# Half of the last additions on POOL, split channel sums for the second half, and row factors transposed later, in one encoder layer

## The chip, the cores and the metric

The kernel runs on one core of a Trainium2 chip. Its engines work side by side, each with its own queue of instructions: TensorE (PE in the profile; its weight loads are PEld), VectorE (DVE), ScalarE (ACT), GpSimd (POOL) and SyncE (SP), which here only issues DMAs. PE writes its products to PSUM, a small memory of banks of 128 x 512 float32; everything else lies in SBUF. POOL takes no part in reading PSUM here.

The metric is the time of one execution in microseconds on the device. Profiled executions have a time of their own.

## The reference

One layer of an encoder for 1024 tokens of 1024 channels, all in float32. The input is normed over its channels and goes through one projection into a pooling branch (u) and into q, k and v of an attention; both branches are gated and merged, projected, normed again and added to the input. A squared-ReLU MLP follows in the same frame:

```python
h = rmsnorm(x, g_pre_mix)
proj = jnp.einsum('bsd,de->bse', h, w_in)            # u_pool | q | k | v
...
mix = jnp.einsum('bsd,de->bse', merged, w_out)
x = x + rmsnorm(mix, g_post_mix)
h2 = rmsnorm(x, g_pre_mlp)
a = jnp.square(jax.nn.relu(jnp.einsum('bsd,df->bsf', h2, w_up)))
ff = jnp.einsum('bsf,fd->bsd', a, w_down)
x = x + rmsnorm(ff, g_post_mlp)
```

`rmsnorm` divides each token by the root of the mean of its squares over the 1024 channels. There are four of these norms, and the change touches all four.

## The kernel before

**Layout.** Activations lie with channels on the partitions: eight tiles of 128 channels by 512 tokens for each half (h = 0 and 1) of the tokens. A product in float32 is made from three products of split operands: a matrix is cast to a shorter type (fp32r) by ACT, the "hi" part, and DVE subtracts it from the original to get the "lo" part; `mm3` (L112 to L114, L110 where an issue order is pinned) multiplies hi by hi, hi by lo and lo by hi. A step of `dense_steps` is three such matmuls of 128 x 512; eight steps make one output tile.

**Norms.** For a norm the squares of the eight channel tiles are added up (acc) and then summed over the partitions by a matmul with a matrix `ones`, all 1/1024 (tile ms). This product is a plain float32 one, which the profile shows as two instructions. `rstd` (L151 to L157) makes the row factor from it: a logarithm and an exponential on ACT and three instructions on DVE. The result is the same in all 128 partitions and goes to `rb[h]`.

**Stage 1** (`phase_in`). Squares and splits of x; then the products of u, groups 0 to 2, for half 0 and then half 1, and group 3 for both halves. The function `stats(h)` makes the row factors (L332 for the sum) and then four transposes of `rb[h]` (L336, tile rt), out of which DVE copies one column each (L337) into `rcol`, the row factors with tokens on the partitions, as v needs them. Both sums and both sets of transposes use a PSUM tile with the tag "o", of which there is one buffer. `stats` is handed to the products of half 1 as side work, `stats(0)` after 2 of their 24 steps and `stats(1)` after 14. After that `u_out` (L380) multiplies the products of u by `rb` on the way out of PSUM; `pool_group` and `pool_mix` make the pooling branch on DVE and PE (tile dm, first half also tag "o"; evicted at L418 and L419). Products for q and k follow, then v (L496, L497), gates and the attention.

**Norm chain** (`chain`, one per half). After the projection of the mixer, each half goes through two norms: sum at L826, scaling and residual (L834, L838), sum at L846, scaling (L851). For half 1 the operands of the MLP are built from the results on DVE and ACT (L877 to L884, L811, L812). It is side work of the first MLP products, whose weights are loaded, cast and split in between (L76, L82, L83).

**Last stage** (`down`). Seven series of products; DVE and ACT split their operands two units ahead (L1091, L1093, L1102). The last norm is in `norm(h, ...)`: sums of `accs` and of the last square (L1200, L1201), row factor, scaling (L1213), residual addition (L1218) and the store (L1219). Half 1 runs as side work beside the series q4 and p2. Half 0 comes last and in two parts of 256 tokens, whose final four products are in `last_tokens`; the second of these parts has nothing beside it any more. The residual of half 0 was loaded ahead into SBUF.

**Order.** The kernel is written for a planner: it traces the instructions, and the planner orders them for each engine by a list schedule in its own model of the time, where the order of the program is the priority. Edges by hand (`issue_after`) fix some orders. Each engine then works its queue off strictly in that order. The constants: `ones` is filled by a memset at the start; then a tile of zeros is filled, from which nine matmuls run ahead of the first real one.

Of the kernel before, what the change touches and what calls it, by code (L numbers as in the profile page):

```python
# [29 lines left out]
P = 128  # L30
H = 512
# [18 lines left out]
class Block:  # L50
# [106 lines left out]
        nc.vector.scalar_tensor_tensor(out=y, in0=b, scalar=-3.0, in1=y, op0=ALU.add, op1=ALU.mult)  # L157
        return y

    def split_gain(self, src, gain, r, hi, lo, pool):  # L160

        nc = self.nc
        n = src.shape[-1]
        f = pool.tile([P, H], F32, name="nf", tag="nf", bufs=4)[:, :n]
        nc.vector.scalar_tensor_tensor(out=f, in0=src, scalar=gain, in1=r, op0=ALU.mult, op1=ALU.mult)
        nc.scalar.copy(hi, f)
        nc.vector.tensor_sub(lo, f, hi.bitcast(F32))

    def build(self):
        tc, nc = self.tc, self.nc  # L170
        self.table_inst = None
        order = [(("u", g), O_U + g) for g in (0, 1, 2, 3)]
        order += [(("q", 0), O_QK), (("k", 0), O_QK + 1)]
        self.fill = {
# [10 lines left out]
        }  # L185
        order += [(("v", 0, j), O_V + j) for j in range(2)]
        for h in range(-1, 9):
            for f in self.fill[h]:
                if f[0] == "v":
                    if f[1] == 0:  # L190
                        order += [(("v", 1, j), O_V + 2 + j) for j in range(2)]
                elif f[0] == "g":
                    if f[-1] != 1 or len(f) == 2:
                        order.append((f[:2], O_G + f[1]))
                else:
                    order.append((f, O_QK + 2 * f[1] + (f[0] == "k")))
        order += [(("br", e), O_BR + e) for e in range(8)]
        kept = {3: "t2_hi", 4: "t2_lo"}
        order += [(("out", 0, e), O_OUT + e, (), None, kept.get(e)) for e in range(8)]
        order += [(("out", 1, e), O_OUT + e) for e in (2, 1, 0)]  # L200
        order += [(("up", i), O_UP + self.pair(i)[0]) for i in range(16)]
        self.set_order(order)

        cp = tc.alloc_tile_pool(name="const", bufs=1, side="left")
        self.wp = tc.alloc_tile_pool(name="weights", bufs=1, side="left")
        self.big = tc.alloc_tile_pool(name="big", bufs=1, side="left")
        dp = tc.alloc_tile_pool(name="scratch", bufs=1, space=DRAM)
        self.gscr = [dp.tile([P, 1024], F32, name=f"gscr{i}") for i in range(16)]
        self.yscr = [[dp.tile([P, 1024], F32R, name=f"yscr{i}_{j}") for j in range(2)] for i in range(4)]
        self.pscr = [[dp.tile([P, 4, H], F32, name=f"pscr{i}_{j}") for i in range(4)] for j in range(2)]  # L210
        self.ascr = [[dp.tile([P, 4, H], F32, name=f"ascr{f}_{h}") for h in range(2)] for f in range(8)]
        self.tscr = [dp.tile([P, 4, H], F32, name=f"tscr{f}") for f in range(4)]
        self.wscr = [[dp.tile([P, 4, 512], F32, name=f"wscr{n}_{q}") for q in range(4)] for n in range(4)]
        self.wsums = self.weight_sums()
        self.xscr = [[dp.tile([P, H], F32, name=f"xscr{h}_{e}") for e in range(8)] for h in range(2)]

        self.vt = cp.tile([P, N_VEC], F32, name="vt")
        nc.scalar.preload_act_table_set(TABLES)
        self.ones = cp.tile([P, P], F32, name="ones")
        nc.vector.memset(self.ones, 1.0 / 1024.0)  # L220
        self.one1 = cp.tile([P, 1], F32, name="one1")
        nc.vector.memset(self.one1, 1.0)
        self.eps = cp.tile([P, 1], F32, name="eps")
        nc.vector.memset(self.eps, EPS)
        self.gn = cp.tile([P, 32], F32, name="gn")
        self.eye = cp.tile([P, P], F32, name="eye")

        self.past = cp.tile([P, 1024], mybir.dt.uint8, name="past")
        self.rcnt = cp.tile([P, 16], F32, name="rcnt")

        self.rp = tc.alloc_tile_pool(name="row", bufs=1, side="left")
        self.rb = [self.rp.tile([P, H], F32, name=f"rb{h}") for h in range(2)]
        self.rcol = cp.tile([P, NK], F32, name="rcol")
        edge = tc.alloc_tile_pool(name="edge", bufs=1, side="right")
        self.edge = edge.tile([P, 24], F32, name="edge")
        self.dps = tc.alloc_tile_pool(name="att_d", bufs=2, space=PSUM)
        self.zps = tc.alloc_tile_pool(name="att_z", bufs=1, space=PSUM)
        self.phase_in()
        self.phase_attention()
        self.phase_post()  # L240
        self.phase_mlp()

        edge.release()
        for p in (self.rp, self.big, self.wp, cp, dp):
            p.release()


    def phase_in(self):
        tc, nc = self.tc, self.nc
        pa = tc.alloc_tile_pool(name="in_a", bufs=1, side="right")  # L250
        xs = [pa.tile([P, NK, H], F32, name=f"x{h}") for h in range(2)]

        def load(h, k, n):
            nc.sync.dma_start(xs[h][:, k : k + n, :], self.x[h][:, k : k + n, :])
# [75 lines left out]
        def stats(h):  # L330
            ms = self.zps.tile([P, H], F32, name="ms", tag="o", bufs=1)
            nc.tensor.matmul(ms, self.ones, accs[h], start=True, stop=True)  # L332
            self.rstd(ms, pa, ("sq", 3), out=self.rb[h])
            rt = self.zps.tile([P, H], F32, name="rt", tag="o", bufs=1)
            for j in range(4):
                nc.tensor.transpose(rt[:, j * P : j * P + P], self.rb[h][:, j * P : j * P + P], self.eye)  # L336
            nc.vector.tensor_copy(  # L337
                self.rcol[:, 4 * h : 4 * h + 4].rearrange("p (j o) -> p j o", o=1),
                rt.rearrange("p (j o) -> p j o", o=P)[:, :, 0:1],
            )  # L340
# [87 lines left out]
        for h in range(2):  # L428
            d = self.dps.tile([P, H], F32, name="du", tag="d")
            self.dense(d, self.weights(("u", 3)), self.hT[h])  # L430
            u_out(3, [(h, d)])
            if h == 0:
                pool_mix(0, pooled[0])
                pooled.append(pool_group(1))
                u_out(2, list(enumerate(dst[2])))
        self.run(self.job_qk("q", 0, 0))
        pool_mix(1, pooled[1])
        pooled.append(pool_group(2))
# [375 lines left out]
    def chain(self, ch, h, mix, acc):  # L814
# [8 lines left out]
        tmp = self.hp.tile([P, 4, H], F32, name=f"tmp{h}", tag="t3_hi")  # L823
        yield 3
        ms = self.ps.tile([P, H], F32, name="ms", tag="ms", bufs=1)
        nc.tensor.matmul(ms, self.ones, acc, start=True, stop=True)  # L826
        r = self.rstd(ms, ch, None, bufs=1, b=tmp[:, 3, :])
        acc2 = ch.tile([P, H], F32, name="acc2", bufs=1)
        for e in range(8):
# [13 lines left out]
                nc.vector.tensor_add(acc2, acc2, sq)  # L843
        yield 28
        ms = self.ps.tile([P, H], F32, name="ms", tag="ms", bufs=1)
        nc.tensor.matmul(ms, self.ones, acc2, start=True, stop=True)  # L846
        self.rstd(ms, ch, None, out=self.rb[h], b=tmp[:, 3, :])

        def norm(e):
# [192 lines left out]
    def down(self):  # L1042
# [149 lines left out]
            nc.gpsimd.dma_start(t, self.xscr[h][e])  # L1192
            return t

        def norm(h, x1, gap, c=slice(0, H), behind=(None,)):

            at = gap
            yield at
            ms = self.ps.tile([P, H], F32, name="ms", tag="ms", bufs=1)[:, c]
            nc.tensor.matmul(ms, self.ones, accs[h][:, c], start=True, stop=False)  # L1200
            nc.tensor.matmul(ms, self.ones, last[h], start=False, stop=True)  # L1201
            r = self.rb[h][:, c]
            self.rstd(ms, mp, ("r", 4), n=c.stop - c.start, out=r)
            nxt = None if x1 else residual(h, 0)
            for e in range(8):
                at += gap
                yield at
                if x1:
                    x = x1[e][:, c]
                else:  # L1210
                    x, nxt = nxt, residual(h, e + 1) if e < 7 else None
                t = ff[h][e][:, c]
                nc.vector.scalar_tensor_tensor(  # L1213
                    out=t, in0=t, scalar=self.gn[:, V_POST_MLP + e : V_POST_MLP + e + 1], in1=r,
                    op0=ALU.mult, op1=ALU.mult,
                )
                with after(behind[0] if e > 2 else None):
                    nc.vector.tensor_add(t, t, x)  # L1218
                (nc.sync if h == 1 or e % 2 or behind[0] else nc.scalar).dma_start(self.out[h, e][:, c], t)  # L1219

        def last_tokens(c, ops, side):
# [50 lines left out]
        side, behind = None, [None]  # L1272
        for c in (slice(0, 256), slice(256, H)):
            last_tokens(c, ops, side)
            side = norm(0, x0, 0, c, behind)
        self.run(side)
        mp.release()

# [47 lines left out]
```

## Time and profile before

| | |
|---|---|
| median of 3 runs | 1290.21 us (1290.13 to 1290.51) |
| profiled execution, its own time | 1291.31 us |
| its span | 1289.5 us |
| instructions | 16851 |
| PE busy | 1268.3 us (98%) |
| DVE busy | 924.2 us (72%) |
| ACT busy | 605.5 us (47%) |
| POOL busy | 175.2 us (14%) |
| mean granted TensorE clock | 0.994 |

A row of a timeline gives the start in us from the beginning of the span, the time it took, engine, line, operation, and the tiles as out<-in with their shapes; rows that follow each other on an engine with the same line are merged, with their number behind an x. In square brackets stands how long the engine was idle before it and what ended that. Rows of the chain of waits have a start, a duration and what the time went to. In the waits view a row names who waited, for whom, the total in us, how often, and the longest. A row of the sums by stretch has the stretch, its length, and then for PE, PEld, DVE, ACT and POOL the busy time with the number of instructions, the granted clock of TensorE, the DMA share and the GB/s. Matmuls overlap in the pipeline, so it is the distance of their starts that counts and not the duration of one.

### The profile page before, as it was taken

The page shows a single profiled execution, that of the slowest core. Times are in us where ns is not written, and L with a number is a line of the kernel's source. Part 1 is how long each engine was busy: PE and PEld are TensorE (multiplying, and loading weights), DVE is VectorE, ACT ScalarE, POOL GpSimd, SP SyncE. Part 2 cuts the span into 40 slices and gives each one's busy share as a digit, 9 for nine tenths or more (in the row PEclk, how much of TensorE's full clock was granted, in tenths as well). Part 3 has the DMA queues.
Part 4 walks back from the last instruction along what each step waited for, and adds up shares of the span by engine and source line. Part 5 has one row for each costly group of instructions (what it writes and reads, how often), then busy time and mean ns, then how long its engine had stood idle before and what let it go on. Part 6 is the DMA issues. An engine that isn't in the chain of part 4 may idle for free.

```text
span 1289.5 us, 16851 instructions
## 1 busy us (share of the span) xinstructions
PE 1268.3 (98%) x6145; PEld 1063.1 (82%) x6145; DVE 924.2 (72%) x1303; ACT 605.5 (47%) x989; POOL 175.2 (14%) x346
## 2 busy tenths in 40 slices
PE   9899999999999999999999999999999999999996
PEld 6688888998888888888877888888888888888885
DVE  8686587688777756661667979777775655776876
ACT  8145455555555543232446646545554433344341
POOL 1011213202322331000101002211220000001000
PEclk9899999999999999999999999999999999999998
DMA  6152646624837978451338577756569546547641
GB/s 223 50 176 81 225 123 164 131 67 113 214 123 177 296 204 234 158 180 49 136 109 285 184 249 254 244 190 210 190 226 342 186 157 225 190 173 246 239 160 66
DMA packets 75746, 233.72 MB, mean 181 GB/s; under 512 B 8624, under 2 KB 11184, under 8 KB 73488
## 3 DMA queue, kind: packets, MB, share of 16 engines
q1 hardware_dynamic: 47936, 143.64, 33.8%
q0 software_dynamic: 27152, 88.49, 23.1%
q8 instruction: 48, 0.79, 0.3%
q10 hardware_dynamic: 576, 0.52, 0.1%
q14 instruction: 34, 0.28, 0.1%
HBM read 178.10 MB, written 83.89 MB: 203 GB/s over the span
## 4 chain that ended last, share of the span: by engine, by line
PE 88%; DVE 6%; DMA 2%; issue 2%; ACT 1%; SPq 0%; POOL 0%; DVEq 0%; POOLq 0%; ACTq 0%
PE d L114 18%; PE d L112 18%; PE d L113 18%; PE dg L110 5%; PE dg L114 5%; PE dg L113 5%; PE o L606 3%; PE at L581 2%; PE dqk L113 2%; PE dqk L114 2%; PE dqk L110 2%; DMA wraw<-w 2%; PE z L552 1%; PE z L549 1%; DVE wlo L83 1%
## 5 line engine op out<-in xcount | busy, mean ns | idle before, releaser
L113 PE MATMUL d<-blo,whi 128*128 128x512 f32 (+1 forms) x456 | 172.7, 379 | 0.0
L114 PE MATMUL d<-bhi,wlo 128*128 128x512 f32 (+1 forms) x456 | 171.9, 378 | 0.0
L112 PE MATMUL d<-bhi,whi 128*128 128x512 f32 (+1 forms) x456 | 168.4, 378 | 0.0
L562 DVE TENSOR_TENSOR_SCAN F<-F,past 128x384 f32<-128x384 f32 (+3 forms) x96 | 93.5, 974 | 25.8 <-ACT F L553 24.9
L82 ACT CAST whi<-wraw 128x512 fp32r<-128x512 f32 (+1 forms) x88 | 67.7, 799 | 88.5 <-PE d L113 33.9
L110 PE MATMUL dg<-hT_hi,whi 128*128 128x512 f32 x256 | 103.3, 404 | 0.3 <-DVE v L497 0.3
L83 DVE TENSOR_TENSOR wlo<-wraw,whi 128x512 fp32r<-128x512 f32 (+1 forms) x88 | 78.2, 907 | 34.1 <-ACT whi L82 34.1
L113 PE MATMUL dg<-hT_lo,whi 128*128 128x512 f32 x256 | 100.6, 393 | 0.0
L114 PE MATMUL dg<-hT_hi,wlo 128*128 128x512 f32 x256 | 100.4, 392 | 0.0
L113 PEld LDWEIGHTS d<-blo,whi 128*128 128x128 f32 x456 | 85.7, 188 | 16.3 <-issue 0.2
L114 PEld LDWEIGHTS d<-bhi,wlo 128*128 128x128 f32 x456 | 85.8, 188 | 16.0 <-issue 0.2
L112 PEld LDWEIGHTS d<-bhi,whi 128*128 128x128 f32 x456 | 85.5, 188 | 15.9
L553 ACT ACTIVATE F<-z 128x384 f32<-128x384 f32 (+3 forms) x96 | 47.3, 493 | 64.1 <-DVE T L566 38.4
L113 PE MATMUL d<-b_lo,whi 128*128 128x512 f32 x196 | 76.7, 391 | 0.0
L112 PE MATMUL d<-b_hi,whi 128*128 128x512 f32 x196 | 75.6, 390 | 0.0
L114 PE MATMUL d<-b_hi,wlo 128*128 128x512 f32 x196 | 75.3, 392 | 0.1
L1093 DVE TENSOR_TENSOR wlo<-slots_hi,whi 128x1024 fp32r<-128x1024 f32 x29 | 35.5, 1224 | 52.6 <-ACT whi L1091 52.5
L1091 ACT CAST whi<-slots_hi 128x1024 fp32r<-128x1024 f32 x29 | 30.5, 1051 | 84.5 <-PE d L113 64.9
L589 DVE TENSOR_TENSOR alo<-at,ahi 128x512 fp32r<-128x512 f32 (+1 forms) x80 | 50.6, 633 | 26.6 <-ACT ahi L588 25.9
L1091 ACT CAST whi<-slots_lo 128x1024 fp32r<-128x1024 f32 x27 | 28.4, 1052 | 72.9 <-PE d L113 59.2
L566 DVE TENSOR_TENSOR T<-T,F 128x127 f32<-128x127 f32 (+4 forms) x96 | 53.1, 556 | 10.2 <-POOL T L556 4.2
L1093 DVE TENSOR_TENSOR wlo<-slots_lo,whi 128x1024 fp32r<-128x1024 f32 x27 | 33.0, 1222 | 36.7 <-ACT whi L1091 36.7
(305 smaller groups left out, 3335.2 us busy)
## 6 DMA issues: line engine op xcount, KB each, us to landing
wraw<-w SPq DMA_DIRECT2D x80, 512.0 KB, 4.3
wscr<-w POOLq DMA_DIRECT2D x24, 1024.0 KB, 9.4
ext_b<-ascr SPq DMA_DIRECT2D x40, 512.0 KB, 4.4
gscr<-gs POOLq DMA_DIRECT2D x32, 256.0 KB, 4.6
gate<-gscr POOLq DMA_DIRECT2D x16, 512.0 KB, 3.7
pscr<-p SPq DMA_DIRECT2D x32, 256.0 KB, 3.7
braw<-w SPq DMA_DIRECT2D x16, 512.0 KB, 5.4
ascr<-c POOLq DMA_DIRECT2D x32, 256.0 KB, 5.2
```

Of the source, the lines that this page charges most:

```text
L82: nc.scalar.copy(hi[:, c], raw[:, c])
L83: self.last_lo = nc.vector.tensor_sub(lo[:, c], raw[:, c], hi[:, c].bitcast(F32)).ins
L110: nc.tensor.matmul(ps, wh, rh, start=first and i == 0, stop=False)
L112: nc.tensor.matmul(ps, wh, rh, start=first and i == 0, stop=False)
L113: nc.tensor.matmul(ps, wh, rl, start=False, stop=False)
L114: nc.tensor.matmul(ps, wl, rh, start=False, stop=last and i == n - 1)
L553: nc.scalar.activation(f[:, c : c + n], z[:, :n], AF.Sigmoid, scale=-1.0)
L562: nc.vector.tensor_tensor_scan(fr, fr, past[:, c : c + n][:, ::-1], 1.0 if top else f[:, c + n : c + n + 1], ALU.mult, ALU.max)
L566: nc.vector.tensor_mul(tl[:, c:e], tl[:, c:e], f[:, c + 1 : e + 1])
L589: nc.vector.tensor_sub(lo[:, c0:], at[:, c0:], hi[:, c0:].bitcast(F32))
L1091: last_split[0] = nc.scalar.copy(hi, src).ins
L1093: last_split[1] = nc.vector.tensor_sub(lo, src, hi.bitcast(F32)).ins
```

## The change

1. The transposes of the row factors and the copies into `rcol` leave `stats(h)` and become `columns(h)`. Both calls stand after the products of u's group 3, ahead of the first product of q.
2. `ones` becomes a tile of type fp32r, filled by a copy from a float32 tile `mean`, so that it serves split products; the float32 products read it through a view. A new helper `channel_sum` casts the sum of squares to hi on ACT, subtracts on DVE for lo, and makes two matmuls with `ones`. For half 1 it takes the place of the float32 product in both norms of the chain and in the last norm; there the last square is first added to the others on DVE, and one sum takes the place of two.
3. In the second part of half 0 of the last norm (`last_part`), the residual additions of tiles 0 to 3 are issued on POOL; those of tiles 4 to 7 stay on DVE. The stores keep their queues: odd tiles on SP, even tiles on ACT in this part.
4. The unused `split_gain` and `one1` (a memset of one column) are gone.

```diff
+    def channel_sum(self, ps, acc, pool, tag, bufs):
+        nc = self.nc
+        hi, lo = (pool.tile([P, H], F32R, name=f"acc_{n}", tag=tag, bufs=bufs) for n in ("hi", "lo"))
+        nc.scalar.copy(hi, acc)
+        nc.vector.tensor_sub(lo, acc, hi.bitcast(F32))
+        nc.tensor.matmul(ps, self.ones_r, hi, start=True, stop=False)
+        nc.tensor.matmul(ps, self.ones_r, lo, start=False, stop=True)
...
-        self.ones = cp.tile([P, P], F32, name="ones")
-        nc.vector.memset(self.ones, 1.0 / 1024.0)
-        self.one1 = cp.tile([P, 1], F32, name="one1")
-        nc.vector.memset(self.one1, 1.0)
+        self.ones_r = cp.tile([P, P], F32R, name="ones")
+        self.ones = self.ones_r.bitcast(F32)
...
+        mean = pa.tile([P, P], F32, name="mean")
+        nc.vector.memset(mean, 1.0 / 1024.0)
+        nc.vector.tensor_copy(self.ones_r, mean)
...
             self.rstd(ms, pa, ("sq", 3), out=self.rb[h])
+
+        def columns(h):
+
             rt = self.zps.tile([P, H], F32, name="rt", tag="o", bufs=1)
...
                 u_out(2, list(enumerate(dst[2])))
+        for h in range(2):
+            columns(h)
         self.run(self.job_qk("q", 0, 0))
...
-        nc.tensor.matmul(ms, self.ones, acc, start=True, stop=True)
+        if h == 0:
+            nc.tensor.matmul(ms, self.ones, acc, start=True, stop=True)
+        else:
+            self.channel_sum(ms, acc, ch, "nf", 2)
...
-        nc.tensor.matmul(ms, self.ones, acc2, start=True, stop=True)
+        if h == 0:
+            nc.tensor.matmul(ms, self.ones, acc2, start=True, stop=True)
+        else:
+            self.channel_sum(ms, acc2, ch, "nf", 2)
...
-            nc.tensor.matmul(ms, self.ones, accs[h][:, c], start=True, stop=False)
-            nc.tensor.matmul(ms, self.ones, last[h], start=False, stop=True)
+            if h == 0:
+                nc.tensor.matmul(ms, self.ones, accs[h][:, c], start=True, stop=False)
+                nc.tensor.matmul(ms, self.ones, last[h], start=False, stop=True)
+            else:
+                nc.vector.tensor_add(accs[h], accs[h], last[h])
+                self.channel_sum(ms, accs[h], mp, "r", 4)
...
-                    nc.vector.tensor_add(t, t, x)
+                    (nc.gpsimd if last_part and e < 4 else nc.vector).tensor_add(t, t, x)
...
-            side = norm(0, x0, 0, c, behind)
+            side = norm(0, x0, 0, c, behind, c.stop == H)
```

More of the change, by code (lines that the diff above doesn't have):

```diff
@@ L158, in rstd @@
         return y
-    def split_gain(self, src, gain, r, hi, lo, pool):
+    def channel_sum(self, ps, acc, pool, tag, bufs):
         nc = self.nc
[L163 to L167, printed above, removed]
+        hi, lo = (pool.tile([P, H], F32R, name=f"acc_{n}", tag=tag, bufs=bufs) for n in ("hi", "lo"))
[3 more added lines that the diff above has]
+        nc.tensor.matmul(ps, self.ones_r, lo, start=False, stop=True)
     def build(self):
@@ L1193, in residual, with norm @@
             return t
-        def norm(h, x1, gap, c=slice(0, H), behind=(None,)):
+        def norm(h, x1, gap, c=slice(0, H), behind=(None,), last_part=False):
             at = gap
```

## The prediction

> **What bounds the kernel now.** I read the page first, then the waits of TensorE alone, then the sums by stretch, then the timelines of the four places that the diff touches.
>
> ```profile
> span 1289.5 us, 16851 instructions
> PE 1268.3 (98%) x6145; PEld 1063.1 (82%) x6145; DVE 924.2 (72%) x1303; ACT 605.5 (47%) x989; POOL 175.2 (14%) x346
> ...
> PE rt L336 <- DVE rb L157: 4.6, 1, 4.6
> PE dv L112 <- DVE v L497: 0.4, 1, 0.4
> ...
> 40.00:50.00 10.00, 5.45 (x19) 3.93 (x19) 5.82 (x9) 2.15 (x3) 0.00 (x0) 0.79 0.29 98
> 50.00:60.00 10.00, 10.00 (x40) 8.05 (x39) 9.86 (x18) 1.05 (x1) 0.00 (x0) 0.87 0.01 2
> ```
>
> TensorE (PE) is busy for 98% of the span, so a microsecond comes off only if a PE wait goes, PE work goes, or the tail behind PE gets shorter. The waits view gives one wait of note: PE stands 4.6 us before the transposes of L336. The stretches around it are the only ones between 10 and 1270 us, of those I summed, with a granted clock under 1.00 (0.79 and 0.87).
>
> **Row factors transposed later.** The timeline, engine by engine:
>
> ```profile
> 29.77 0.69 DVE L155 SCALAR_TENSOR_TENSOR nb<-ms,rb 128x512 f32<-128x512 f32 x1
> 30.37 0.68 DVE L328 TENSOR_TENSOR acc<-acc,sq 128x512 f32<-128x512 f32 x1
> 36.38 0.60 PE L336 MATMUL rt<-eye,rb 128*128 128x128 f32 x4
> 37.02 0.16 DVE L337 COPY rcol<-rt 128x4 f32<-128x4 f32 x1 [3.50 <-PE rt L336]
> 41.40 1.02 PE L332 MATMUL ms<-acc,ones 128*128 128x512 f32 x2
> 42.50 0.40 PE L114 MATMUL zu<-hT_hi,wlo 128*128 128x512 f32 x1
> 46.70 0.69 DVE L157 SCALAR_TENSOR_TENSOR rb<-nb,rb 128x512 f32<-128x512 f32 x1
> 47.31 1.28 DVE L380 TENSOR_TENSOR u<-du,rb 128x512 f32<-128x512 f32 x2
> 47.45 1.11 PE L336 MATMUL rt<-eye,rb 128*128 128x128 f32 x4 [4.55 <-DVE rb L157]
> 48.21 0.77 PE L112 MATMUL du<-hT_hi,whi 128*128 128x512 f32 x1
> 52.63 0.40 PE L113 MATMUL du<-hT_lo,whi 128*128 128x512 f32 x1
> 52.87 0.40 PE L114 MATMUL du<-hT_hi,wlo 128*128 128x512 f32 x1
> ```
>
> Taking the transposes out of PE's queue would alone bring almost nothing: the next matmul, du at 48.21, needs the bank that L380 frees at about 47.31 + 0.65 = 47.96, and L380 waits for the same row factor rb of half 1. What helps is the PSUM bank. Tiles ms and rt share one (tag "o", one buffer), so now half 1's sum at 41.40 has to come behind the copy of half 0's transposes (37.02), though its data were complete at 30.37 + 0.68 = 31.05. Without rt in between, the bank is free when L155 has read ms, at 30.46. Then only the program position holds the sum: step 14 of the 24 steps of half 1, so 30 matmuls before their end. At 0.23 us each (the last two rows lie 0.24 apart) these are 6.9 us, with the sum's own 0.86, counted back from 42.73 with half 0's transposes (about 0.35 of PE's time) gone: 42.4 - 7.8 = 34.6.
>
> From the sum's start to the finished rb now pass 46.70 + 0.69 - 41.40 = 6.0 us, with a weight cast and split among them. Then rb stands at 40.6 and the bank is freed at 41.3, a microsecond before PE asks for it at 42.4. So du starts at 42.4 and not 48.21: 5.8 us. The slow clock goes with the wait: ten intervals from 48.21 to 52.63 took 4.42 us, at 0.23 they take 2.3, so 2.1 more. The eight transposes come later at 0.35 per four (0.7). PE gains 5.8 + 2.1 - 0.7 = 7.2. DVE, which is full from 68 to 95 us, starts its evictions 47.39 - 40.6 = 6.8 earlier and gets the two copies of 0.16 there: 6.5. PE waits for DVE at the end of that stretch (the 0.4 of L497), so the smaller number counts: **-6.5** (bounds -4.5, a sum planned 2 us later, and -7.2). No DMA moves in this edit; POOL's and SP's queues in the stretch keep their order and come earlier with DVE and ACT.
>
> The new place has a price of its own: the first of the moved products must wait until pool_mix(0)'s product leaves bank "o", the second for the first copy. Nobody needs rcol until the first v, past 90 us, and the planner has the q and k products to put in front. I cost it at nothing; the fourth rival is what it costs without that cover.
>
> **Channel sums of half 1 as split products.**
>
> ```profile
> 663.19 0.91 PE ms L826 x2
> 703.24 1.02 PE L846 MATMUL ms<-acc,ones 128*128 128x512 f32 x2
> 1196.99 0.86 PE ms L1200 x2
> 1197.85 0.86 PE ms L1201 x2
> ...
> 677.05 1.23 DVE L83 TENSOR_TENSOR wlo<-wraw,whi 128x1024 fp32r<-128x1024 f32 x1 [6.06 <-ACT whi L82]
> 711.29 0.62 ACT L811 CAST b_hi<-mix 128x512 fp32r<-128x512 f32 x1 [2.06 <-DVE mix L851]
> 716.35 0.69 DVE L812 TENSOR_TENSOR b_lo<-mix,b_hi 128x512 fp32r<-128x512 f32 x1
> 740.55 4.37 DMA wraw<-w
> 749.29 1.24 DVE wlo L912
> 1216.84 1.22 DVE L1093 TENSOR_TENSOR blo<-ext_b,bhi 128x1024 fp32r<-128x1024 f32 x1
> 1220.35 0.39 PE L113 MATMUL d<-blo,whi 128*128 128x512 f32 x1
> ```
>
> A sum in plain float32 costs PE 0.86 us; as two split products 2 x 0.23 = 0.46. The two of the chain give 2 x 0.4 = 0.8, those of the last norm (two sums become one) 1.72 - 0.46 = 1.26. Each pays with a cast on ACT (0.62) and a subtraction on DVE (0.69), one behind the other, so its result comes 1.3 - 0.4 = 0.9 us later (the two halves take buffers, nf and r, that squares had left by then); the last norm also gets an addition of 0.69. The first sum's delay falls into 6.06 us in which DVE waits for a weight cast. The second (703.24) sits ahead of the 33 us in which DVE makes the operands, and at their end DVE frees the weight buffer whose load and split PE needs at 750.5, with a few hundredths of slack. There the 0.8 can be eaten and up to 0.9 lost: bounds -0.8 and +0.9; I take **-0.2**. In the last norm DVE gets 1.4 us more and PE comes 1.3 sooner; the closest operand is ready at 1216.84 + 1.22 = 1218.06 and used at 1220.35, a margin of 2.3 against 2.7. Bounds -1.26 and +0.4; I take **-0.9**, because the planner may place the splits earlier again.
>
> **Half of the last part's additions on POOL.**
>
> ```profile
> 1280.48 3.26 DVE L1213 SCALAR_TENSOR_TENSOR ff<-ff,gn,rb 128x256 f32<-128x256 f32 x8
> 1283.65 1.43 DVE L1218 TENSOR_TENSOR ff<-ff,slots_hi 128x256 f32<-128x256 f32 x4
> 1284.99 1.43 DVE L1218 TENSOR_TENSOR ff<-ff,slots_lo 128x256 f32<-128x256 f32 x4
> ...
> 4.10 1.03 POOL L297 TENSOR_SCALAR_AFFINE_SELECT past<-past 128x1024 f32<-128x1024 f32 x1
> 135.30 0.29 POOL L556 TENSOR_SCALAR_AFFINE_SELECT T<-T 128x128 f32<-128x128 f32 x1 [0.61 <-ACT T L554]
> 137.16 1.21 DVE L562 TENSOR_TENSOR_SCAN F<-F,past 128x512 f32<-128x512 f32 x1
> 137.37 1.09 POOL L556 TENSOR_SCALAR_AFFINE_SELECT T<-T 128x128 f32<-128x128 f32 x1 [1.78 <-ACT T L554]
> ```
>
> The tail is DVE alone: eight multiplications, eight additions at 0.34 each, ending at 1286.42, then the stores. Four additions off DVE give 4 x 0.34 = 1.34 if POOL runs beside it. But the same POOL operation takes 0.29 alone and 1.09 at 137.37, and there it ends at 138.46, just behind the scan that DVE ends at 138.37. That scan reads two SBUF tensors, and so do the multiplications and the additions of the tail. If they keep each other out, the sum of both engines' work sets the end. The trace has no two-input POOL operation; from 0.29 for 128 and 1.03 for 1024 elements, 256 cost an estimated 0.40 with one input and, the data part doubled, 0.6 with two. The end then moves by 4 x (0.6 - 0.34) = +1.0. Bounds: -1.3 (side by side) and +1.5 (0.7 each). I take **+0.8**, nearer to the row with the scan. New is also that the stores of tiles 0 to 3 wait for POOL, tile 1 and 3 on SP's queue and 0 and 2 on ACT's, and a late one holds the stores queued behind it, those of tiles 4 to 7; as both engines then end about together, nothing is added for that. The Trainium skill, GPSIMD Engine Reference (Key points; Performance versus the Vector engine), says that POOL shares its SBUF interfaces with VectorE and collides with instructions of two SBUF inputs, and that a two-input addition of 2048 elements takes it 4497 ns. By that figure 256 elements cost an estimated 0.56 us and the tail +0.9; the trace agrees on the collision and shows no such addition.
>
> **The start.**
>
> ```profile
> 0.90 0.17 DVE L220 MEMSET ones<- 128x128 f32 x1 [0.90 <-PEq L1317]
> 1.41 3.80 PE L307 MATMUL idle<-zero 128*128 128x512 bf16 x9 [1.41 <-DVE zero L304]
> ```
>
> One more small DVE operation, about 0.17, stands ahead of the zero tile that PE's first products wait for; these end at 5.21, shortly before the first real ones. **+0.1** (0 to +0.2).
>
> **The sum.** -6.5 - 0.2 - 0.9 + 0.8 + 0.1 = -6.7. The profiled execution took 1291.31 us for a span of 1289.5, so 1284.6 on its own scale; the median of the runs is 1290.21, 1.1 lower, and there the forecast is 1283.5.
>
> **The rivals.**
>
> The stall stays. Half 1's sum is planned late again, or its cast waits, and PE waits for L380's bank instead of the transposes: du then comes at 47.96 in place of 48.21, the slow clock stays, and that term is -0.3. Sum -0.5, 1289.7. For it: L380 hangs on the same rb, and a planner's order is not read from the source. Against: the shared bank explains 37.02 to 41.40, and it is gone.
>
> POOL runs beside DVE. Tail -1.3 in place of +0.8: 1281.4. For it: at 135.30 POOL is undisturbed; against: 137.37.
>
> The splits are paid in full: DVE's weight splits come late at 750 and 1220, +0.9 and +0.4 in place of -0.2 and -0.9: 1285.9; with the additions' worst +1.5 in the tail, 1286.6.
>
> The moved transposes block PE (slower).
>
> ```profile
> 61.30 0.39 PE L112 MATMUL dqk<-hT_hi,whi 128*128 128x512 f32 x1
> 66.99 1.41 DVE L419 SCALAR_TENSOR_TENSOR u<-dm,vt,win 128x512 fp32r<-128x512 f32 x2 [3.40 <-ACT win L418]
> ```
>
> PE leaves u at 61.30, and pool_mix(0)'s product leaves bank "o" only when L419 has read it, from 66.99 on. Were the transposes put directly behind u, PE would stand 5.7 + 0.7 us, with 2.1 of slow clock behind it: 8.5; the second set waits for a copy in a full DVE queue, priced like today's wait, 4.55 + 2.1 = 6.7. Together +15.2: -6.7 + 15.2 = +8.5, 1298.7. It decides once the two waits and their slow clock pass 6.7 us. Against it: at 36.38 the planner set the first transposes between matmuls without a wait.
>
> **How the numbers follow.** Forecast 0.60 (1281.8 to 1285.6), stall stays 0.12, POOL beside 0.10, splits paid 0.13, blocked 0.04, something not listed 0.01. The likeliest is 1283.5. Up to 1290 the range takes in the stall that stays, and it starts at 1280.4, a microsecond under the POOL rival, for the -7.2 and -0.8 bounds. This kernel's runs can tell about 0.2% (2.6 us) from no change: faster means under 1287.6. The forecast, the POOL rival and most of the paid splits lie there: 0.82. Same, from the stall that stays and the rest: 0.13. Slower: 0.05.
>
> **What would show it.** The wait of PE for rb at L336 gone and the clock at 1.00 between 40 and 60; half 1's first sum near 35 and du near 42.4. The sums at L826, L846 and L1200 as pairs 0.23 apart, and no new PE wait at 750 or near 1220. In the tail POOL additions longer than 0.6 that end with DVE's instructions, the last work later than the 5.94 us from the first multiplication. I am wrong if du still waits for L380, if PE waits for rt, or if the POOL additions take under 0.34 each beside an unslowed DVE.

## The result, and the profile after

The changed kernel took 1297.10 us (median of 6 runs, 1296.88 to 1298.05), the kernel before on the same chip 1290.36 (6 runs, 1289.94 to 1292.05): 1.0052 times as long, 95% interval 1.0039 to 1.0065. It is slower by 6.7 us where the prediction had it faster by 6.7; that the two sizes agree is chance. The reason is in none of the edits that the prediction weighed: it is the removal of the constant `one1`, 4 bytes in each partition, which the prediction did not mention.

The head of the page of the changed kernel, and its waits view of TensorE:

```profile
span 1295.2 us, 16855 instructions
PE 1278.1 (99%) x6143; PEld 1060.0 (82%) x6143; DVE 927.2 (72%) x1303; ACT 608.1 (47%) x992; POOL 178.8 (14%) x350
```

```profile
PE idle L308 <- DVE zero L305: 1.4, 1, 1.4
PE d L112 <- DVE oT L619: 0.9, 1, 0.9
PE ms L1213 <- DVE acc L1254: 0.8, 1, 0.8
...
PE d L113 <- DVE b_lo L818: 0.4, 1, 0.4
```

The wait of 4.6 us for rb is gone and nothing of its size has come in its place. Yet PE is busy for 9.8 us more, with two products fewer. So the products themselves take longer. First, what came as forecast: the sums by stretch and the timeline of the changed kernel around the old stall (columns as in the prediction).

```profile
40.00:50.00 10.00, 10.00 (x45) 8.29 (x45) 9.97 (x17) 1.05 (x1) 0.00 (x0) 1.00 0.28 102
50.00:60.00 10.00, 10.00 (x45) 8.26 (x44) 7.19 (x12) 2.29 (x3) 0.00 (x0) 1.00 0.17 54
```

```profile
34.85 1.02 PE L333 MATMUL ms<-acc,ones 128*128 128x512 f32 x2
40.28 0.69 DVE L157 SCALAR_TENSOR_TENSOR rb<-nb,rb 128x512 f32<-128x512 f32 x1
40.89 1.28 DVE L384 TENSOR_TENSOR u<-du,rb 128x512 f32<-128x512 f32 x2
42.10 0.39 PE L112 MATMUL du<-hT_hi,whi 128*128 128x512 f32 x1
67.34 0.60 PE L340 MATMUL rt<-eye,rb 128*128 128x128 f32 x4
74.40 0.60 PE L340 MATMUL rt<-eye,rb 128*128 128x128 f32 x4
```

The second half's sum runs at 34.85 (forecast 34.6), rb is done at 40.97 (40.6), and du starts at 42.10 (42.4). The clock is 1.00 where it was 0.79 and 0.87. The transposes stand among the products of q, without a wait. The first product of q starts at 52.98, against 61.30 before: 8.3 us earlier.

Now the loss. Of the two tiles behind the arrow of a product, the first is the moving one (128x512 here) and the second the stationary one, the weights, whose loads the profile shows as PEld. Three stretches without a wait follow, first of the kernel before and then of the changed one. The first holds products of the mixer's operands (yh, oh), the second products of b, the third products of the last stage (bhi, blo), all with weights from whi and wlo:

```profile
490.00:560.00 70.00, 70.00 (x310) 57.96 (x309) 45.95 (x63) 18.31 (x23) 6.86 (x13) 1.00 0.58 180
700.00:730.00 30.00, 30.00 (x132) 24.45 (x132) 26.04 (x38) 20.85 (x32) 0.00 (x0) 1.00 0.61 195
1000.00:1100.00 100.00, 100.00 (x443) 82.84 (x442) 59.50 (x55) 40.23 (x42) 0.00 (x0) 1.00 0.56 194
```

```profile
490.00:560.00 70.00, 70.00 (x302) 56.23 (x301) 46.04 (x65) 16.04 (x21) 6.86 (x13) 1.00 0.47 153
700.00:730.00 30.00, 30.00 (x134) 24.83 (x133) 28.28 (x42) 20.19 (x34) 0.00 (x0) 1.00 0.64 191
1000.00:1100.00 100.00, 100.00 (x430) 80.33 (x429) 57.33 (x52) 37.64 (x40) 0.00 (x0) 1.00 0.55 188
```

In the last stretch PE is busy throughout at clock 1.00 in both kernels, and does 430 products in place of 443. The median distance of two starts is 227 ns before and 234 after. The first stretch shows the same, 302 against 310. The second does not: products of b with these weights kept their pace (before, the float32 sum at 703.24 stands in this stretch, two instructions that take 0.86 us). The slow ones are scattered over the stages but have something in common, which the built program's allocation shows. The kernel fills SBUF from two sides. On the left lie the constants, behind them the weights (whi, wlo) and hT, mg, b0, b1 (one place, reused). On the right lie yh and yl, oh and ol, t, the weights shi and slo, bhi and blo. Before, all these tiles started at 128 modulo 256 bytes. `one1` took a slot of 32 bytes among the constants; without it everything behind them on the left starts at 96, and the right side stays at 128. The groups at 233 to 234 ns are those with one operand from each side. Groups with both operands from the left (hT, mg, b with whi) stayed at 227. In the shorter products of 128x256 no loss shows: the 144 with bhi or blo and weights from whi and wlo have a median distance of 120 ns before and 117 after.

The tail, of the changed kernel, with the DRAIN rows of the program's last line (instruction and count, then shortest, median and longest in ns, and the first and last start; POOL's longest is its first):

```profile
1285.52 5.12 DVE L1229 SCALAR_TENSOR_TENSOR ff<-ff,gn,rb 128x256 f32<-128x256 f32 x8
1286.09 3.47 POOL L1235 TENSOR_TENSOR ff<-ff,slots_hi 128x256 f32<-128x256 f32 x4 [54.44 <-DVE ff L1229]
1290.56 1.42 DVE L1235 TENSOR_TENSOR ff<-ff,slots_lo 128x256 f32<-128x256 f32 x4
```

```profile
L1339 POOLq DRAIN  x3: 51/102/6016, 1288.2 to 1294.7; - x3
L1339 SPq DRAIN  x3: 7/7/7, 1294.0 to 1294.4; - x3
```

From the first multiplication to the end of the span it is 1295.2 - 1285.52 = 9.7 us, before it was 1289.5 - 1280.48 = 9.0: 0.7 more (forecast 0.8). The eight multiplications took 5.12 in place of 3.26: each of POOL's four additions kept DVE out for (5.12 - 3.26) / 4 = 0.47. One addition on POOL every 0.86 us (below) is this 0.47 and the 0.40 from one undisturbed multiplication to the next, as if the two engines took turns.

### The profile page after: what moved, and what is told of

Read it like the earlier page. It is cut to its first block, busy times and chain, and to the rows that moved or that the text cites. A ratio compares the mean times of both kernels' runs of the same rounds, so it can differ in the third digit from the quotient of the medians.

```text
span 1295.2 us, 16855 instructions
## 1 busy us (share of the span) xinstructions
PE 1278.1 (99%) x6143; PEld 1060.0 (82%) x6143; DVE 927.2 (72%) x1303; ACT 608.1 (47%) x992; POOL 178.8 (14%) x350
## 4 chain that ended last, share of the span: by engine, by line
PE 98%; DVE 1%; DMA 0%; ACT 0%; SPq 0%; issue 0%; DVEq 0%
PE d L113 20%; PE d L114 20%; PE d L112 20%; PE dg L114 5%; PE dg L110 5%; PE dg L113 5%; PE o L612 3%; PE at L587 2%; PE dqk L114 2%; PE dqk L113 2%; PE dqk L110 2%; PE z L558 1%; PE z L555 1%; PE dv L113 1%; PE dv L114 1%; PE dv L112 1%
```

## The experiments

| kernel | median us | kernel before, same chip | ratio, 95% interval |
|---|---|---|---|
| changed, one1 back | 1280.92 | 1290.36 | 0.9926, 0.9912 to 0.9939 |
| before, without one1 | 1306.83 | 1290.36 | 1.0125, 1.0111 to 1.0138 |
| changed, right side moved too | 1280.72 | 1290.36 | 0.9922, 0.9909 to 0.9936 |
| before, left moved by 64 bytes | 1305.92 | 1290.68 | 1.0119, 1.0102 to 1.0136 |
| before, left moved by 128 | 1306.21 | 1290.13 | 1.0122, 1.0106 to 1.0139 |
| before, left moved by 256 | 1290.59 | 1290.87 | 0.9996, 0.9987 to 1.0006 |
| before, only hT, mg, b moved | 1304.05 | 1290.68 | 1.0105, 1.0090 to 1.0120 |
| one1 back, transposes in `stats` | 1288.72 | 1290.68 | 0.9986, 0.9977 to 0.9995 |
| one1 back, float32 sums | 1282.62 | 1290.68 | 0.9937, 0.9923 to 0.9952 |
| one1 back, no addition on POOL | 1280.06 | 1290.36 | 0.9918, 0.9904 to 0.9931 |
| one1 back, all eight on POOL | 1284.15 | 1290.22 | 0.9955, 0.9941 to 0.9969 |
| one1 back, none on POOL, half 0's chain sums split | 1283.10 | 1290.22 | 0.9947, 0.9933 to 0.9961 |

**The constant put back.**

```diff
+        self.one1 = cp.tile([P, 1], F32, name="one1")
+        nc.vector.memset(self.one1, 1.0)
```

> The changed kernel with the one-column constant one1 and its memset restored, nothing else. All is computed as in the changed kernel. It puts the buffers that lie behind the constants in SBUF (weights, hT, mg, b0, b1, the slots) back by 32 bytes, to where they lay in the kernel before. Theory A (TensorE's products run slower when moving and stationary tile lie at different offsets modulo 128 bytes; the changed kernel moved one side only): the distance of starts in the groups at 233 ns falls back to 227 ns, and the time is that of the kernel before less what the stall and the sums gave, -8.0 - 2.1 + 0.6 = -9.5: about 1280.9. Rival B (the slow products come from the new order of the work or from the split sums, and not from addresses): nothing changes, about 1297.

1280.92, as theory A had it. The stretch of the last stage has 443 products again:

```profile
1000.00:1100.00 100.00, 100.00 (x443) 82.77 (x442) 61.93 (x59) 38.56 (x41) 0.00 (x0) 1.00 0.54 185
```

Between this kernel and the changed one, the distances behind the 2280 products of 128x512 with one operand from each side differ by 14.9 us in all, 6.6 ns each, and those behind the 2416 with both from one side by 1.4. The spans differ by 1295.2 - 1279.3 = 15.9, so these products are nearly the whole loss.

**The constant taken out of the kernel before.**

```diff
-        self.one1 = cp.tile([P, 1], F32, name="one1")
-        nc.vector.memset(self.one1, 1.0)
```

> The kernel before with only one1 and its memset taken out; everything is computed. Theory A: the products of tiles from the shifted side with tiles from the other side go from 227 to 233 ns, as in the changed kernel; about 15 us more, 1305. Rival B: a memset of one column less changes nothing, 1290.4.

1306.83, 16.5 us slower by these two lines alone, in a kernel whose work and order are otherwise the old ones. Rival B, that the new order or the split sums make the slow products, falls.

**Both sides moved.** In the changed kernel, on the other side of SBUF:

```diff
-        self.edge = edge.tile([P, 24], F32, name="edge")
+        self.edge = edge.tile([P, 32], F32, name="edge")
```

> The changed kernel, one1 still gone, but a small tile on the other side of SBUF (edge) is 32 instead of 24 columns wide, so that the buffers of that side move by 32 bytes as well and both sides lie at the same offset modulo 128 bytes again, 96. The order of the instructions stays and everything is computed. Theory A, with the offset of the two operands to each other deciding: 227 ns everywhere, about 1281. Theory A', with each address on its own deciding (a start that isn't a multiple of 128 bytes is slow): all products slow, above 1297. Rival B: 1297.

1280.72. All tiles now start at 96 modulo 256, the order of the instructions on every engine is that of the changed kernel, and the 16 us are gone, without one1:

```profile
1000.00:1100.00 100.00, 100.00 (x443) 82.81 (x442) 61.65 (x59) 38.66 (x41) 0.00 (x0) 1.00 0.54 186
```

So the start of a tile is not slow in itself (theory A'). The offset of the two operands to each other decides.

**How far they may be apart.** The kernel before, with one1 widened:

```diff
-        self.one1 = cp.tile([P, 1], F32, name="one1")
+        self.one1 = cp.tile([P, 24], F32, name="one1")
```

> The kernel before with one1 24 instead of 1 column wide; everything is computed. The buffers behind the constants (weights, hT, mg, b0, b1, the slots) move by 64 bytes, to 64 modulo 128, and those of the other side stay at 0. Theory A with a period of 128 bytes: products of tiles from the two sides are slow, as with the offset of 96, about 1306.8. Theory A with a period of 64 bytes: nothing changes, 1290.4. An offset of 64 may also cost another amount than one of 32; then the distance in these groups tells it.

```diff
-        self.one1 = cp.tile([P, 1], F32, name="one1")
+        self.one1 = cp.tile([P, 40], F32, name="one1")
```

> The kernel before with one1 40 instead of 1 column wide; everything is computed. The buffers behind the constants move by 128 bytes: to 0 modulo 128 against the other side, and to 128 modulo 256. If the offset of the two operands counts modulo 128 bytes: 227 ns everywhere, 1290.4. If it counts modulo 256: slow as with 32 and 64 bytes, 1304 to 1307.

```diff
-        self.one1 = cp.tile([P, 1], F32, name="one1")
+        self.one1 = cp.tile([P, 72], F32, name="one1")
```

> The kernel before with one1 72 instead of 1 column wide; everything is computed. The buffers behind the constants move by 256 bytes. In the kernel before, the distance between the buffers of the two sides is a multiple of 256 bytes; a move by 128 already made the products of the two sides slow. If the distance counts modulo 256 bytes: 227 ns everywhere, 1290.4. If it counts modulo more than that, or any move costs: 1304 to 1307.

Slow, slow and not slow: 1305.92, 1306.21 and 1290.59. Moves by 64 and by 128 bytes cost about what the 32 bytes do, and a move by 256 costs nothing. The expectations of the first runs speak of 128 bytes, and that was wrong: the offset counts modulo 256.

**Another pair of operands.** In the kernel before, a buffer of 32 bytes between the weights and hT, mg, b0, b1:

```diff
         self.wp = tc.alloc_tile_pool(name="weights", bufs=1, side="left")
+        self.gap = tc.alloc_tile_pool(name="gap", bufs=1, side="left")
+        nc.vector.memset(self.gap.tile([P, 1], F32, name="gap1"), 1.0)
         self.big = tc.alloc_tile_pool(name="big", bufs=1, side="left")
```

> The kernel before with a buffer of 32 bytes between the weights and the operands hT, mg, b0 and b1 (and a memset of one column in it); everything is computed. Weights and the other side stay at 0 modulo 128, those operands move to 32. Theory A (relative offset): now hT, mg and b with the weights are slow, and b with the weights of the other side, about 2360 products x 6.6 ns = 15.6 us, while oh, t and bhi with the weights stay at 227 ns, although these were slow in the changed kernel: about 1306. If the place of the weights alone decided: 1290.4. If the other side's place alone decided: 1290.4.

1304.05, 13.4 us over the kernel before, some 2 us less than the 15.6 expected. The trace shows where: the 768 products of the gates (dg) grew by 3.6 ns on average and the 384 of q and k (dqk) by 4.5, in place of 6.6; why is open. The groups change places as theory A says. Its sums by stretch, to be set beside those of the changed kernel above, and a piece of its timeline:

```profile
700.00:730.00 30.00, 30.00 (x129) 23.78 (x128) 23.85 (x34) 20.45 (x32) 0.54 (x1) 1.00 0.72 249
1000.00:1100.00 100.00, 100.00 (x443) 82.83 (x442) 55.51 (x49) 38.48 (x41) 0.00 (x0) 1.00 0.56 199
```

```profile
766.88 0.39 PE L114 MATMUL d<-t_hi,wlo 128*128 128x512 f32 x1
767.11 0.39 PE L112 MATMUL d<-t_hi,whi 128*128 128x512 f32 x1
767.33 0.39 PE L113 MATMUL d<-t_lo,whi 128*128 128x512 f32 x1
767.56 0.39 PE L114 MATMUL d<-t_hi,wlo 128*128 128x512 f32 x1
767.78 0.40 PE L114 MATMUL d<-b_hi,wlo 128*128 128x512 f32 x1
768.02 0.39 PE L112 MATMUL d<-b_hi,whi 128*128 128x512 f32 x1
768.25 0.40 PE L113 MATMUL d<-b_lo,whi 128*128 128x512 f32 x1
768.49 0.40 PE L114 MATMUL d<-b_hi,wlo 128*128 128x512 f32 x1
```

Now b is the slow one (129 products in 30 us in place of 132) and bhi is back at 443. Within two microseconds, with weights from the same buffers, four distances from the first product of t take 0.90 us (766.88 to 767.78, 0.225 each) and the three of b behind them 0.71 (767.78 to 768.49, 0.237 each). The products of hT with the weights, which no other kernel here made slow, have a median of 234 ns. So it is not the place of the weights nor of one side, but the pair.

**The transposes back.**

```diff
             self.rstd(ms, pa, ("sq", 3), out=self.rb[h])
-
-        def columns(h):
-
...
-        for h in range(2):
-            columns(h)
```

> The changed kernel with one1 restored and the transposes of the row factors back in the statistics of each half, as in the kernel before; everything is computed. From the traces (start of the first product of q 8.3 us earlier in the changed kernel, 8.0 left at 482 us): 8.0 us over the kernel with one1 alone restored, about 1288.9. By the size that the prediction gave the stall: 6.5, about 1287.4. If the stall was not the transposes' doing: 1280.9.

1288.72, 7.8 over the kernel with one1 back (between the two traces it is 8.3 at the first product of q and stays at about 8.5 to the end). The wait is there again:

```profile
PE rt L339 <- DVE rb L157: 4.5, 1, 4.5
```

**The float32 sums back.**

```diff
-            self.channel_sum(ms, acc, ch, "nf", 2)
+            nc.tensor.matmul(ms, self.ones, acc, start=True, stop=True)
...
-                nc.vector.tensor_add(accs[h], accs[h], last[h])
-                self.channel_sum(ms, accs[h], mp, "r", 4)
+            nc.tensor.matmul(ms, self.ones, accs[h][:, c], start=True, stop=False)
+            nc.tensor.matmul(ms, self.ones, last[h], start=False, stop=True)
```

> The changed kernel with one1 restored and the three sums of half 1 as float32 products again, as in the kernel before; everything is computed. If all of TensorE's saving counts (0.85 and 1.26): 2.1 over the kernel with one1 alone restored, 1283.0. By the prediction's -0.2 and -0.9: 1.1, 1282.0. If the split sums cost what they save: 1280.9.

1282.62, 1.7 over the kernel with one1 back, between the two sizes. In the two traces the last sum on PE starts 1.75 us later with float32 sums, though that run came into the middle of the program 0.4 earlier, which makes 2.15. By place, the two sums of the chain give 0.8 and those of the last norm 1.3. The split sums are worth about 2 us, and nearly all of PE's saving counts.

**No addition on POOL.**

```diff
-                    (nc.gpsimd if last_part and e < 4 else nc.vector).tensor_add(t, t, x)
+                    nc.vector.tensor_add(t, t, x)
```

> The changed kernel with one1 restored and all additions of the last part on VectorE; everything is computed. Theory A: as with one1 restored alone, and the tail shorter by the 0.5 us that POOL beside VectorE costs: about 1280.3. If POOL's additions cost nothing, the same as with one1 restored alone (1280.9). Rival B: 1296.5.

1280.06, the fastest of all. POOL's additions cost 0.9 by the medians. The tail in this kernel's trace:

```profile
1268.97 3.26 DVE L1231 SCALAR_TENSOR_TENSOR ff<-ff,gn,rb 128x256 f32<-128x256 f32 x8
1272.14 1.43 DVE L1237 TENSOR_TENSOR ff<-ff,slots_hi 128x256 f32<-128x256 f32 x4
1273.48 1.43 DVE L1237 TENSOR_TENSOR ff<-ff,slots_lo 128x256 f32<-128x256 f32 x4
```

The multiplications are back at 3.26, and from the first of them to the end of the span (1277.9) it is 8.9 us, 0.7 less than with POOL.

**All eight on POOL.**

```diff
-                    (nc.gpsimd if last_part and e < 4 else nc.vector).tensor_add(t, t, x)
+                    (nc.gpsimd if last_part else nc.vector).tensor_add(t, t, x)
```

> The changed kernel with one1 restored and all eight additions of the last part on POOL; everything is computed. It shows what a POOL addition takes once VectorE has run out of work. If the two engines keep each other out and an addition holds SBUF for (5.12 - 3.26) / 4 = 0.47 us, by which VectorE's multiplications were stretched per addition: 3.26 + 8 x 0.47 = 7.0 from the first multiplication to the last addition, against 6.46 with four on POOL, so about 1281.4, the last POOL additions 0.47 each. If an addition takes POOL 0.87 us by itself, as it took beside VectorE: 0.6 + 8 x 0.87 = 7.6, about 1282.0, all at 0.87.

1284.15, 3.2 over the kernel with four on POOL. Both expectations are too small by over 2 us. The timeline and the DRAIN rows of this kernel:

```profile
1269.12 6.06 DVE L1231 SCALAR_TENSOR_TENSOR ff<-ff,gn,rb 128x256 f32<-128x256 f32 x8
1269.69 3.48 POOL L1237 TENSOR_TENSOR ff<-ff,slots_hi 128x256 f32<-128x256 f32 x4 [53.20 <-DVE ff L1231]
1273.13 3.30 POOL L1237 TENSOR_TENSOR ff<-ff,slots_lo 128x256 f32<-128x256 f32 x4
```

```profile
L1341 POOLq DRAIN  x3: 51/93/5773, 1275.3 to 1281.6; - x3
L1341 SPq DRAIN  x3: 7/7/7, 1278.2 to 1281.3; - x3
```

POOL's additions follow each other at 0.86 us, (1273.13 - 1269.69) / 4, and end at 1276.43, 7.3 after the first multiplication; that is near the second expectation's 7.6. DVE lost 6.06 - 3.26 = 2.8 to them, which is 0.47 for each of the six multiplications that the trace shows stretched (0.94 each in place of 0.48). The last addition, which began when DVE had finished, took 0.72 where those beside DVE took 0.90. What costs most stands behind them, and neither expectation had it. SP, which waits for the stores, is through at 1278.2, but POOL's DRAIN at the end of the program lasts until 1275.3 + 5.77 = 1281.05: 4.6 us behind its last addition, and 2.8 behind the stores. In the changed kernel it is 4.6 as well (1294.2 against 1286.09 + 3.47 = 1289.56), and there it ends 0.2 behind SP's. In the kernel without additions on POOL, where the last work of POOL is the issue of DMAs at 1215, it was over by 1224.4, long before the stores. What the DRAIN does in those 4.6 us the traces do not show.

**Half 0's sums split too**, in the fastest kernel:

```diff
-        if h == 0:
-            nc.tensor.matmul(ms, self.ones, acc, start=True, stop=True)
-        else:
-            self.channel_sum(ms, acc, ch, "nf", 2)
+        self.channel_sum(ms, acc, ch, "nf", 2)
```

and the same for acc2.

> The changed kernel with one1 restored, all additions of the last part on VectorE, and now half 0's two sums of the norm chain as split products too; everything is computed. If half 0's sums pay as half 1's did (0.85 for the two): 0.8 under the same kernel without them, 1279.2. If the longer way to half 0's row factor holds up what follows: 1280.1 to 1281.

1283.10, 3.0 slower than without it, more than either case allowed. Its waits and the timeline of PE:

```profile
PE d L112 <- ACT b_hi L819: 2.4, 1, 2.4
```

```profile
653.85 0.73 PE L112 MATMUL d<-b_hi,whi 128*128 128x512 f32 x2 [2.40 <-ACT b_hi L819]
```

Half 0's row factor has no slack: the first MLP product waits for the operand made from it, 2.4 us, against the 0.8 saved. That is 1.6 of the 3.0. A further 1.3 of the difference between the two traces was there at 52 us already, where TensorE's order is the same in both (2.4 - 0.8 + 1.3 = 2.9; the spans differ by 1280.9 - 1277.9 = 3.0). Whether the unprofiled runs had those 1.3 as well is not known; the wait alone is shown.

## Why the prediction was wrong

**The step that failed** is the sum's list of terms: "-6.5 - 0.2 - 0.9 + 0.8 + 0.1 = -6.7" prices three of the four parts of the change and a small operation at the start; the fourth part, the removal of `one1`, is not among them: it stands at nothing, without a reason. Behind it stands the sentence that "a microsecond comes off only if a PE wait goes, PE work goes, or the tail behind PE gets shorter", and the 0.23 us taken as the price of a product whatever its operands' places. In the products of 128x512 nothing was expected to change, so 3% more in 2280 of them (14.9 us at 6.6 ns each) had no term. By the runs the missing term is +16.2 (1297.10 - 1280.92) for tiles of one side moved by 32 bytes against those of the other. None of the rivals, the slower one included, was this, and the page of the kernel before could not have shown it: there the pace was the same everywhere.

**The stall** was right in mechanism, in every time forecast for it to within 0.4 us, and larger than taken: 7.8 by the runs against 6.5, and over its bound of 7.2. Of PE's 8.3 us at 53, 8.0 were left at 482 us. So PE's larger number (7.2 forecast) was the one that counted, not DVE's 6.5: the evictions that DVE has to do in the full stretch did not hold PE back, and the 0.4 us that PE waited for v went too (it is in the run with the transposes back, and not in the changed kernel's waits). The moved transposes, whose waits were taken as nothing, show none.

**The split sums** were given -0.2 and -0.9 and brought 1.7 together by the medians, and by the traces 0.8 and 1.3, the favourable end of both bounds. "There the 0.8 can be eaten" did not happen: the weights at 750 and the operands at 1218 came in time. What came late instead is b_lo for 0.4 us in the changed kernel's waits.

**POOL in the tail** was +0.8 and is +0.7 by the two spans, +0.9 by the medians. The mechanism was the forecast one, both engines' work added up; the number came out by luck, since the sizes were off in two directions that cancel. An addition keeps DVE out for 0.47 and not 0.6, so DVE's last addition ends 4 x (0.47 - 0.34) = 0.5 later behind the first multiplication, and the stores, by SP's first DRAIN, 0.3 later. The other 0.4 lies behind the stores, at the end of the program: POOL's DRAIN ends 0.2 after SP's, and the steps behind it take another 0.2. The prediction added nothing there. The addition itself takes POOL 0.86 us beside DVE. The Trainium skill, GPSIMD Engine Reference (Performance versus the Vector engine), gave by its figure for 2048 elements an estimated 0.56, so for 256 elements the measurement beside DVE is longer by half, and the one addition without DVE (0.72) by over a quarter; the measurement decides.

**The start** was given +0.1 for one more DVE operation ahead of the zero tile. There is none: the memset of `one1` is gone, and the copy into `ones` runs behind the memset of zero (1.29 against 1.10). PE's first product starts at 1.43 where it started at 1.41.

Put together by the runs: -7.8 - 1.7 + 0.9 + 16.2 = +7.6, against +6.7 measured; the medians that are subtracted here have ranges of 1 to 2 us, and they come from several chips, on which the kernel before took 1290.13 to 1290.87. By the traces it is -8.5 - 2.1 + 0.7 + 15.9 = +6.0, and the spans differ by 1295.2 - 1289.5 = 5.7.

What stays open is what in the chip does it. The runs show that the pair of the moving and the loaded tile decides, modulo 256 bytes, and that 32, 64 and 128 bytes apart cost about the same. Whether the moving tile has to match its own weights or those of the next product, they do not separate, as both usually lie in the same buffers. Only where one group follows another do the two differ. In the changed kernel's trace 18 products have their own weights apart and the next ones matching, with a median distance of 233 ns, and 17 the other way round, with 235; in the kernel moved by 64 bytes the same places have 233 and 226. So neither pairing alone accounts for all of it.

## What to carry to other kernels

A kernel that is bound by TensorE has an operand layout among its inputs: when any tile is added, removed or resized ahead of others in SBUF, however small, print where the operands of the large products start, and keep moving and stationary tiles at the same offset modulo 256 bytes; a resized dummy tile does it. In the profile the sign is a busy PE at full clock, without waits, with fewer products in a stretch than before (430 in place of 443 in 100 us), in some pairs of tiles only. Before an edit is costed at nothing because its instruction is nothing, ask what else it held in place: here the removal of 4 bytes cost more than the other three parts brought.

## What the runs showed of the hardware that was not expected

- Products of 128x512 in fp32r follow each other at 227 ns when moving and stationary tile start at the same offset modulo 256 bytes, and at 233 ns on average (medians 232 to 234) when they are 32, 64 or 128 bytes apart, at a granted clock of 1.00. In this kernel that is 13 to 16 us of 1290. Products of 128x256 showed no loss (120 and 117 ns).
- A POOL addition of two SBUF tiles of 128x256 takes 0.86 us beside DVE, and holds off DVE's multiplications, which read two SBUF tiles, for 0.47 us of it. The one that ran without DVE took 0.72.
- POOL's DRAIN at the end of the program ended 4.6 us after POOL's last addition, with four additions there as with eight. With eight it ended 2.8 us behind the stores.
